# S5 chunk inputs in two products of 64 state columns instead of one of 128

## The chip, the cores and the metric

One core of a Trainium2 chip runs the whole program in one launch. The metric is the device time of one execution in microseconds (us), the median of several. The tensor engine (PE) multiplies a stationary operand that is loaded into it (the loads are shown as PEld) with a moving one and writes to PSUM. The vector engine (DVE), the scalar engine (ACT) and GpSimd (POOL) work elementwise, SyncE (SP) mostly issues DMAs.

## The reference, cut to what matters

Four decoder layers follow each other: S5, gated linear attention, differential attention, Mamba-2. The change touches the token mixer of the first, a diagonal complex state space model with 128 groups of 16 channels and 64 states. It runs over 256 tokens in chunks of 64.

```python
ug = u.reshape(bsz, nc, S5_CHUNK, S5_GROUPS, S5_GROUP)...
def chunk_step(carry, u_c):
    h_re, h_im = carry
    dr = jnp.einsum('tbgh,gph->tbgp', u_c, bb_re)
    di = jnp.einsum('tbgh,gph->tbgp', u_c, bb_im)
    pr, pim, sr, si = lax.associative_scan(_complex_affine_combine, (a_re, a_im, dr, di), axis=0)
    sr = sr + pr * h_re - pim * h_im
    si = si + pr * h_im + pim * h_re
    y = jnp.einsum('tbgp,ghp->tbgh', sr, c_re) - jnp.einsum('tbgp,ghp->tbgh', si, c_im)
    return (sr[-1], si[-1]), y
...
g = jax.nn.gelu(y)
out = g * jax.nn.sigmoid(g @ w_glu) * jax.nn.silu(z)
```

## The kernel before

The kernel works with chunks of four tokens: the inputs of a chunk, weighted with powers of the transition, give what the chunk adds to the state (the chunk input); the state at the chunks' starts follows from a recurrence over 64 chunks, and the outputs from the inputs within a chunk (matrix `tm`) and the state at its start (`E`). All of it is done in full fp32, which PE takes in two passes: every matmul in the code is two records in the trace.

The 2048 channels are worked through in four units of 512 (`s5_unit(ub)`), each in two parts, ahead of the `yield` and behind it. Ahead of it stand, for each of four sub-blocks `sb`:

- `scaled` on DVE (L651 to 656) makes the weighted input matrix `bu`; four ACT copies (L668) spread it into a padded tile `bpp`; eight PE transposes (L673) and two ACT copies (L674) make the stationary matrix `pm`, 128 x 128 for each of two complex parts `c` and four `g`;
- PE multiplies it with the inputs `V` (128 x 64) into `dps`, the chunk inputs, for two complex parts and four `g` (L678, eight matmuls, 16 records);
- three ACT copies (L681) put `dps` into `E`, in the order in which the recurrence reads it.

`psc` (L641) turns the output matrices once in a unit, with stationary operands of 64 columns, and ACT copies them into `ct` (L643). Then for each sub-block `cu` (DVE, one buffer) is copied to `cp` (ACT, L691), PE makes the output kernel `kps` (L695), and DVE and ACT copy it into `kt` (L698, L699). Sixteen DMAs on SP (L703) place the pieces of `kt` in `tm`. DVE then runs the recurrence over `E`: ten steps (L712 to 715) and eight large operations (L727 to 730). Behind the `yield` PE computes `y` from `V` and `tm` (L741) and from `E` and `cp` (L745), and ACT applies gelu (L747).

Between the two parts of a unit a list of other work is taken up, the fill: the input projection (L226), which makes the `V` of the later units (DVE transposes, L791), the gate and the queries. Its matmuls have 512 moving columns where weights stand still, 256 otherwise. A scheduler that gives each instruction a priority and follows estimated times sets the order on every engine; the parts of the units have a raised priority. Each engine then executes its list strictly in this order. PSUM buffers limit it: `ps` has three (shared by `psc`, transposes, `dps`, `kps`), `ps2` (for `y`) one, `acc` (fill) two. Behind the last unit the next projection starts (L228), which first needs fp32r halves of the normalised input (`hhi`, L821; `pr`, L822); `pr` reuses space that the last `y` matmuls read.

Of the kernel before, what the change touches and what calls it, by code (L numbers as in the profile page):

```python
# [37 lines left out]
class Net:  # L38
# [571 lines left out]
    def s5_unit(self, ub, V, p, tab, fix, gT):  # L610

        nc, a = self.nc, self.a
# [25 lines left out]
        for c in range(2):  # L638
            for r in range(4):
                for h in range(2):  # L640
                    nc.tensor.matmul(psc[64 * h:64 * h + 64, c, r, :], cnat[:, c, r, :], idv[:, :, h, :],  # L641
                                     start=True, stop=True)
        nc.scalar.copy(ct.rearrange("p r c g h -> p c r (g h)"), psc)  # L643

        def scaled(dst, src, tb, k, conj):

            sv = bc(src.rearrange("p c g h -> p (c g) h"), 2, 4)
            w1, w2 = (t_([P, 2, 4, 4, 16], f"q{i}") for i in range(2))
            for i, t in enumerate((w1, w2)):
                pw = tb[:, i, :, k].rearrange("p e c g -> p (c g) e")  # L650
                vec.tensor_tensor(t.rearrange("p c g e h -> p (c g) e h"), sv, bc(pw, 3, 16), MUL)  # L651
            vec.tensor_tensor(dst[:, 0], w1[:, 0], w2[:, 1], SUB)
            if conj:
                vec.scalar_tensor_tensor(dst[:, 1], w1[:, 1], -1.0, w2[:, 0], MUL, SUB)
            else:
                vec.tensor_tensor(dst[:, 1], w1[:, 1], w2[:, 0], ADD)
# [3 lines left out]
        for sb in range(4):  # L660
            l0 = 4 * sb
            ls = slice(l0, l0 + 4)
            bu = t_([P, 2, 4, 4, 16], "bu", 2)
            bpp = bpps[sb % 2]
            scaled(bu, bt[:, sb], pwb, 4 * ub + sb, False)
            for c in range(2):
                for ps_, hs_ in halves:
                    nc.scalar.copy(bpp[ps_, c, :, :, hs_], bu[ps_, c])  # L668
            pm = t_([P, 2, 4, P], "pm", 2)
            for c in range(2):  # L670
                tp = self.ps().rearrange("p (g x) -> p g x", g=4)
                for g in range(4):
                    nc.tensor.transpose(tp[:, g, :], bpp[:, c, g].rearrange("p s x -> p (s x)"), self.ident)  # L673
                nc.scalar.copy(pm[:, c], tp)  # L674
            dps = self.ps().rearrange("p (c g j) -> p c g j", c=2, g=4)
            for c in range(2):
                for g in range(4):
                    nc.tensor.matmul(dps[:, c, g, :], pm[:, c, g, :], V[:, :, l0 + g, :], start=True, stop=True)  # L678

            for d, s, n in ((32, 0, 32), (8, 32, 24), (1, 56, 7)):  # L680
                nc.scalar.copy(E[:, :, ls, d:d + n], dps[:, :, :, s:s + n])  # L681

        kt = t_([P, 4, P], "kt")
        for sb in range(4):
            l0 = 4 * sb
# [47 lines left out]
        for sb in range(4):  # L733
            l0 = 4 * sb
# [4 lines left out]
            for t in range(4):  # L739
                for g in range(4):  # L740
                    nc.tensor.matmul(y[32 * g:32 * g + 32, t, :], tm[:, l0 + g, 32 * t:32 * t + 32], V[:, :, l0 + g, :],  # L741
                                     start=True, stop=False)
                for c in range(2):
                    for g in range(4):
                        nc.tensor.matmul(y[32 * g:32 * g + 32, t, :], cp[:, c, g, t, :], E[:, c, l0 + g, :],  # L745
                                         start=False, stop=c == 1)
# [813 lines left out]
```

## Time and profile before

| | |
|---|---|
| runs | 1404.85, 1398.51, 1406.41 us; median 1404.85 |
| profiled execution | 1399.02 us, span 1397.0 us |
| PE busy | 1339.7 us, 96% of the span |
| PEld busy | 1089.2 us, 78% |
| DVE busy | 979.5 us, 70% |
| ACT busy | 765.3 us, 55% |
| POOL busy | 122.6 us, 9% |

The profiled execution is 5.83 us below the median of the runs. The S5 units run from about 38 to 237 us of the span. In the rows further below a time is counted from the start of the span, a busy time includes the tail of a group, so that consecutive rows of PE overlap a little, and what stands in brackets is idle time of the engine ahead of the row and what ended it.

### The profile page before, as it was taken

Reading aid. Unit: us, or ns where it says so; the run is one execution under the profiler, and the core shown is the slowest. Engines: PE = TensorE matmul, PEld = TensorE weight load, DVE = VectorE, ACT = ScalarE, POOL = GpSimd, SP = SyncE. Lnnn points to the kernel's source line nnn. Section 1 sums busy time; section 2 is a strip of 40 time slices with the busy share of each in tenths; the row PEclk is TensorE's granted clock in tenths of the full one; section 3 lists DMA queues with packets and bytes.
Section 4 is the critical chain, followed back from the end, with each engine's and each line's share of the span. In section 5 each row is a group of like instructions: output and inputs, shape, how many; then the busy total and the mean of one; then the engine's idle time right before and its main releaser. Section 6 shows DMA issues by size and latency. Waiting matters only on the chain. (4 is left out here: it accounts for less than half of the span.)

```text
span 1397.0 us, 24146 instructions
## 1 busy us (share of the span) xinstructions
PE 1339.7 (96%) x9482; PEld 1089.2 (78%) x9482; DVE 979.5 (70%) x1807; ACT 765.3 (55%) x1336; POOL 122.6 (9%) x153
## 2 busy tenths in 40 slices
PE   6999999999999899999999999999899999999998
PEld 3675667899988787786887777777777898888976
DVE  7689787876547577665467687676766587777873
ACT  2674543565543576554456566566555466665652
POOL 1320000010002100001012021102002000000000
PEclk9999999999999899999999999999999999999999
DMA  5444134565655465444655544344335454444342
GB/s 176 93 103 141 46 95 159 188 183 150 188 186 179 121 180 153 123 150 123 197 168 182 161 129 147 129 141 152 106 121 163 131 151 137 142 146 136 128 144 76
DMA packets 175666, 199.86 MB, mean 143 GB/s; under 512 B 32329, under 2 KB 112450, under 8 KB 175554
## 3 DMA queue, kind: packets, MB, share of 16 engines
q1 hardware_dynamic: 173442, 193.72, 45.5%
q10 hardware_dynamic: 1280, 3.21, 0.7%
q0 software_dynamic: 832, 1.41, 0.7%
q8 instruction: 74, 1.21, 0.4%
q14 instruction: 38, 0.31, 0.1%
HBM read 194.64 MB, written 1.05 MB: 140 GB/s over the span
## 5 line engine op out<-in xcount | busy, mean ns | idle before, releaser
L115 DVE TENSOR_TENSOR lo<-raw,hi 128x1024 fp32r<-128x1024 f32 x331 | 400.4, 1214 | 220.8 <-ACT hi L114 220.1
L114 ACT CAST hi<-raw 128x1024 fp32r<-128x1024 f32 x331 | 343.6, 1040 | 377.7 <-PE acc L230 229.3
L228 PE MATMUL acc<-hi,hT 128*128 128x512 f32 (+1 forms) x576 | 232.9, 404 | 1.9 <-ACT v L947 1.2
L230 PE MATMUL acc<-hi,hT 128*128 128x512 f32 (+1 forms) x576 | 227.8, 396 | 1.5 <-DVE hT L118 1.3
L229 PE MATMUL acc<-lo,hT 128*128 128x512 f32 (+1 forms) x576 | 227.3, 395 | 0.0
L107 POOL TENSOR_TENSOR rr<-rv,mhalf 128x2 f32<-128x2 f32 (+3 forms) x34 | 69.4, 2042 | 1020.5 <-DVE rv L105 970.4
L228 PEld LDWEIGHTS acc<-hi,hT 128*128 128x128 f32 x576 | 109.8, 191 | 29.0 <-issue 3.4
L230 PEld LDWEIGHTS acc<-hi,hT 128*128 128x128 f32 x576 | 109.5, 190 | 27.6 <-DVE hT L118 2.7
L229 PEld LDWEIGHTS acc<-lo,hT 128*128 128x128 f32 x576 | 109.6, 190 | 22.1 <-issue 0.2
L228 PE MATMUL ps<-hT,hi 128*128 128x256 f32 (+1 forms) x328 | 96.4, 294 | 3.9 <-DVE hT L118 1.4
L230 PE MATMUL ps<-hT,lo 128*128 128x256 f32 (+1 forms) x328 | 95.1, 290 | 0.1
L229 PE MATMUL ps<-hT,hi 128*128 128x256 f32 (+1 forms) x328 | 95.1, 290 | 0.0
L226 PE MATMUL acc<-raw,hT 128*128 128x512 f32 x160 | 76.8, 612 | 0.0
L228 PE MATMUL ps<-ghi,hi 128*128 128x256 f32 x256 | 72.6, 284 | 0.7 <-ACT xt L421 0.7
L229 PE MATMUL ps<-glo,hi 128*128 128x256 f32 x256 | 71.8, 281 | 0.0
L230 PE MATMUL ps<-ghi,lo 128*128 128x256 f32 x256 | 71.8, 281 | 0.0
L228 PEld LDWEIGHTS ps<-hT,hi 128*128 128x128 f32 (+1 forms) x328 | 63.0, 192 | 6.9 <-issue 2.1
L228 PE MATMUL acc<-hT,hi 128*128 128x256 f32 x224 | 64.7, 289 | 2.0 <-ACT xq L469 1.2
L230 PEld LDWEIGHTS ps<-hT,lo 128*128 128x128 f32 (+1 forms) x328 | 63.0, 192 | 1.3 <-issue 0.4
L230 PE MATMUL acc<-hT,lo 128*128 128x256 f32 x224 | 63.8, 285 | 0.0
L229 PEld LDWEIGHTS ps<-hT,hi 128*128 128x128 f32 (+1 forms) x328 | 63.0, 192 | 0.7 <-issue 0.2
L229 PE MATMUL acc<-hT,hi 128*128 128x256 f32 x224 | 63.5, 284 | 0.0
(481 smaller groups left out, 2802.6 us busy)
## 6 DMA issues: line engine op xcount, KB each, us to landing
raw<-in_w_out_dram SPq DMA_DIRECT2D x80, 512.0 KB, 3.7
raw<-in_diff_w_in_dram SPq DMA_DIRECT2D x72, 512.0 KB, 3.7
raw<-in_ssd_w_in_dram SPq DMA_DIRECT2D x56, 512.0 KB, 4.0
raw<-in_gla_w_in_dram SPq DMA_DIRECT2D x48, 512.0 KB, 3.7
raw<-in_s_w_in_dram SPq DMA_DIRECT2D x40, 512.0 KB, 4.8
raw<-in_w_mem_kv_dram SPq DMA_DIRECT2D x32, 512.0 KB, 4.0
raw<-in_s_w_glu_dram SPq DMA_DIRECT2D x32, 512.0 KB, 3.8
tm<-kt SPq DMA_DIRECT2D x16, 64.0 KB, 2.1
```

The lines of the kernel that those rows point to most:

```text
L107: nc.gpsimd.tensor_tensor(r, v, self.mhalf[:, :n], ALU.pow)
L114: nc.scalar.copy(hi, src)
L115: nc.vector.tensor_tensor(lo, src, hi.bitcast(F32), SUB)
L226: mm(out, s[0], m[0], start=start, stop=stop)
L228: mm(out, s[0], m[0], start=start, stop=False)
L229: mm(out, s[0], m[1], start=False, stop=False)
L230: mm(out, s[1], m[0], start=False, stop=stop)
```

## The change

Each of the eight matmuls that make `dps` becomes two, each with half of the 128 state columns of `pm` as its stationary operand, and into half of the partitions of `dps`. The sums are the same. In the four units 128 matmuls become 256, in records 256 become 512.

```diff
             dps = self.ps().rearrange("p (c g j) -> p c g j", c=2, g=4)
             for c in range(2):
                 for g in range(4):
-                    nc.tensor.matmul(dps[:, c, g, :], pm[:, c, g, :], V[:, :, l0 + g, :], start=True, stop=True)
+                    for q in (0, 64):
+                        nc.tensor.matmul(dps[q:q + 64, c, g, :], pm[:, c, g, q:q + 64], V[:, :, l0 + g, :],
+                                         start=True, stop=True)
```

The scheduler makes another order of all engines' work from it, from the second sub-block of unit 0 to the end of unit 3; behind that, and in the other three layers, the orders are equal. Lines behind L678 are two further down in the changed kernel. Numbers in names tell buffers apart.

PE in unit 0, around the first two sub-blocks (`ps_430`, `ps_466` or `ps_474` are `dps`, the other `ps` are transposes), before:

```order
L226 MATMUL acc_717<-raw_353,hT_134 128x512
L678 MATMUL ps_430<-V_355,pm_417 128x64 x8
L673 MATMUL ps_454<-ident,bpp_304 128x128 x4
L673 MATMUL ps_460<-ident,bpp_304 128x128 x4
L226 MATMUL acc_717<-raw_353,hT_134 128x512
L678 MATMUL ps_466<-V_355,pm_453 128x64 x8
```

and now:

```order
L226 MATMUL acc_749<-raw_353,hT_134 128x512
L679 MATMUL ps_430<-V_355,pm_417 64x64 x16
L673 MATMUL ps_462<-ident,bpp_304 128x128 x4
L673 MATMUL ps_468<-ident,bpp_304 128x128 x4
L226 MATMUL acc_749<-raw_353,hT_134 128x512
L679 MATMUL ps_474<-V_355,pm_461 64x64 x16
```

Here only the shape is another, and the count; the order is the same. From unit 1 on the sixteen often stand in two groups of eight with a fill matmul between them.

PE in unit 1, behind the chunk inputs: `kps` of the third sub-block (from `cp_291`; `acc` is fill), before:

```order
L695 MATMUL ps_1192<-cp_290,bpad 32x128 x4
L226 MATMUL acc_767<-hT_134,raw_740 128x256
L695 MATMUL ps_1192<-cp_290,bpad 32x128 x4
L226 MATMUL acc_767<-hT_134,raw_740 128x256 x2
L226 MATMUL acc_1329<-hT_119,raw_763 128x256
L695 MATMUL ps_1214<-cp_291,bpad 32x128 x8
L226 MATMUL acc_1329<-hT_119,raw_763 128x256 x3
```

and now:

```order
L697 MATMUL ps_1256<-cp_290,bpad 32x128
L226 MATMUL acc_1393<-hT_134,raw_797 128x256
L697 MATMUL ps_1256<-cp_290,bpad 32x128
L226 MATMUL acc_1393<-hT_134,raw_797 128x256 x2
L226 MATMUL acc_1393<-hT_119,raw_795 128x256 x4
L226 MATMUL acc_1393<-hT_134,raw_797 128x256 x4
L697 MATMUL ps_1278<-cp_291,bpad 32x128 x3
L226 MATMUL acc_1415<-hT_119,raw_1389 128x256
L697 MATMUL ps_1278<-cp_291,bpad 32x128
L226 MATMUL acc_1415<-hT_119,raw_1389 128x256
L697 MATMUL ps_1278<-cp_291,bpad 32x128
```

Its eight matmuls stood together, three fill matmuls behind the `kps` before it; now ten fill matmuls are ahead of its first, and one between each of the next. On DVE the copy of this `kps` into `kt` stands in the midst of unit 0's recurrence.

PE in unit 3, around the last `kps` (from `cp_292`), before:

```order
L678 MATMUL ps_2330<-V_1966,pm_2317 128x64 x8
L695 MATMUL ps_2354<-cp_289,bpad 32x128 x8
L695 MATMUL ps_2376<-cp_290,bpad 32x128 x8
L695 MATMUL ps_2398<-cp_291,bpad 32x128 x8
L695 MATMUL ps_2420<-cp_292,bpad 32x128
L226 MATMUL acc_2509<-raw_1952,hT_119 128x512
L695 MATMUL ps_2420<-cp_292,bpad 32x128
```

and now (`ps_258_2065` and `ps_259_2164` are `y` of unit 2):

```order
L226 MATMUL acc_2933<-hT_134,raw_2660 128x256
L697 MATMUL ps_2548<-cp_292,bpad 32x128
L743 MATMUL ps_258_2065<-V_1462,tm_302 32x64 x4
L747 MATMUL ps_258_2065<-E_294,cp_299 32x64 x8
...
L747 MATMUL ps_258_2065<-E_294,cp_299 32x64 x8
L697 MATMUL ps_2548<-cp_292,bpad 32x128 x7
L226 MATMUL acc_2933<-hT_134,raw_2660 128x256
L743 MATMUL ps_259_2164<-V_1462,tm_302 32x64 x4
```

The last `kps` of unit 3 moved behind the first half of unit 2's `y`. The fill that stood between unit 3's `y` matmuls is now all ahead of them.

ACT at the third sub-block of unit 3, before:

```order
L681 COPY E_295<-ps_2258 128x2x4x7
L674 COPY pm_2281<-ps_2282 128x512
L674 COPY pm_2281<-ps_2288 128x512
L681 COPY E_295<-ps_2294 128x2x4x32
L681 COPY E_295<-ps_2294 128x2x4x24
L681 COPY E_295<-ps_2294 128x2x4x7
```

and now:

```order
L683 COPY E_295<-ps_2362 128x2x4x7
L674 COPY pm_2393<-ps_2394 128x512
L693 COPY cp_290<-cu_2493 64x16x16
L469 COPY xq_2662<-acc_2637 128x1024
L674 COPY pm_2393<-ps_2400 128x512
L693 COPY cp_291<-cu_2515 64x16x16 x3
L683 COPY E_295<-ps_2406 128x2x4x32
L683 COPY E_295<-ps_2406 128x2x4x24
L683 COPY E_295<-ps_2406 128x2x4x7
```

All sixteen `cp` copies of unit 3 stood ahead of its first `E` copies; now they lie between them.

## Rows read from the trace of the kernel before

**Rows 1.** Busy time by stretch; stretch, length, then busy (count) per engine.
```profile
core 0: us, PE busy (x) PEld busy (x) DVE busy (x) ACT busy (x) POOL busy (x), PEclk, DMA share, GB/s
...
90.20:121.30 31.10, 31.10 (x201) 20.85 (x200) 30.50 (x70) 16.04 (x39) 2.11 (x3) 1.00 0.40 113
...
sum 188.80, PE 183.34 PEld 129.44 DVE 153.01 ACT 97.89 POOL 16.55; mean PE 18.33 PEld 12.94 DVE 15.30 ACT 9.79 POOL 1.66
```

**Rows 2.** Timeline of PE, unit 0: start, us, engine, line, operation, count.
```profile
52.00 1.89 PE L678 MATMUL ps<-V,pm 128*128 128x64 f32 x16
```

**Rows 3.** Timeline of all engines, unit 2: `psc` with columns of 64.
```profile
99.65 1.01 PEld L641 LDWEIGHTS ps<-ident,cnat 128*64 128x64 f32 x32 [0.20 <-issue]
99.65 1.15 PE L641 MATMUL ps<-ident,cnat 128*64 128x64 f32 x32
```

**Rows 4.** Timeline of ACT, unit 0: copies of the second chunk input.
```profile
53.93 0.70 ACT L681 COPY E<-ps 128x256 f32<-128x256 f32 x3
```

**Rows 5.** Timeline of all engines, end of unit 1's chunk inputs.
```profile
89.04 0.70 ACT L681 COPY E<-ps 128x256 f32<-128x256 f32 x3 [0.33 <-PE ps L678]
...
89.75 0.40 ACT L691 COPY cp<-cu 64x256 f32<-64x256 f32 x1
...
90.19 0.42 DVE L652 TENSOR_TENSOR cu<-q,q 128x256 f32<-128x256 f32 x1 [5.42 <-ACT cp L691]
```

**Rows 6.** Timeline of PE: fill alone, and fill with single `kps` matmuls between.
```profile
105.45 7.50 PE L226 MATMUL acc<-hT,raw 128*128 128x256 f32 x34
...
195.06 0.41 PE L695 MATMUL ps<-cp,bpad 128*32 128x128 f32 x2
195.39 1.13 PE L226 MATMUL acc<-raw,hT 128*128 128x512 f32 x2
196.45 0.41 PE L695 MATMUL ps<-cp,bpad 128*32 128x128 f32 x2
```

**Rows 7.** Timeline of DVE: recurrences of units 0 and 3.
```profile
120.37 0.96 DVE L730 TENSOR_TENSOR E<-E,fx 128x784 f32<-128x784 f32 x1
...
210.26 0.69 DVE L712 TENSOR_TENSOR sa<-E,s5tw 128x512 f32<-128x512 f32 x1
...
211.98 0.62 DVE L712 TENSOR_TENSOR sa<-E,s5tw 128x448 f32<-128x448 f32 x1
...
222.75 0.97 DVE L730 TENSOR_TENSOR E<-E,fx 128x784 f32<-128x784 f32 x1
```

**Rows 8.** Timeline of PE: unit 1's `y`, unit 3's first chunk input, the end.
```profile
159.95 0.32 PE L745 MATMUL ps<-E,cp 128*32 128x64 f32 x8
160.08 0.29 PE L741 MATMUL ps<-V,tm 128*32 128x64 f32 x8
...
160.42 0.29 PE L741 MATMUL ps<-V,tm 128*32 128x64 f32 x8
...
180.11 1.89 PE L678 MATMUL ps<-V,pm 128*128 128x64 f32 x16
...
232.84 2.86 PE L226 MATMUL acc<-hT,raw 128*128 128x256 f32 x12
...
236.73 0.38 PE L228 MATMUL ps<-hhi,hi 128*128 128x256 f32 x1 [1.03 <-ACT hi L114]
```

**Rows 9.** Timeline of ACT, unit 3: the last copies into `E`.
```profile
192.46 0.70 ACT L681 COPY E<-ps 128x256 f32<-128x256 f32 x3 [1.79 <-PE ps L678]
```

**Rows 10.** Groups by line, ACT, 47 to 237 us; count, busy, mean ns.
```profile
L691 ACT COPY cp<-cu 64x256 f32<-64x256 f32 x64 | 25.8, 403 | 18.8 <-PE ps L745 11.4 <-DVE cu L652 6.5
...
L674 ACT COPY pm<-ps 128x512 f32<-128x512 f32 x31 | 17.3, 606 | 0.4 <-PE ps L673 0.2
```

**Rows 11.** Timeline of SP: DMAs into `tm` of units 1 and 2.
```profile
111.73 10.69 SPq L703 DMA_DIRECT2D tm<-kt  x16
...
170.62 13.12 SPq L703 DMA_DIRECT2D tm<-kt  x16
```

**Rows 12.** Line L703 (all 64 DMAs into `tm`): from issue to landing.
```profile
DMA to landing us min/median/max: 1.8/2.1/3.8
```

## The prediction, made before the result was known

> **What bounds the kernel now.** I read the busy time by stretch first. From 47.9 to 236.7 us, where the changed matmuls lie, PE is busy 183.3 of 188.8 us [rows 1], so it idles 5.5 us. DVE is no bystander: from 90.2 to 121.3 us it is busy 30.5 of 31.1 us, as full as PE, on unit 0's recurrence and on the inputs of units 1 and 2 [rows 1]. ACT is third, but within the chunk inputs of a unit it is the full one: in unit 0 it starts its copies out of `dps` at 53.93 without a wait ahead of them [rows 4]. PE is filled up with work that may run at any time. So a busy PE doesn't yet say that PE sets the end: shorter work on PE moves the end only where a copy on ACT and a recurrence on DVE move with it. The end of the stage is the chain of unit 3: last copy into `E`, recurrence, `y`, fill, next projection at 236.73 [rows 7 to 9]. All behind it has the same order before and after, so I price the change by the shift of this one start.
>
> **The matmuls alone.** The sixteen records of one sub-block take 1.89 us [rows 2]. The changed shape occurs already: `psc` has stationary operands of 64 columns and 64 moving ones, and 32 of its records take 1.15 us [rows 3]. The saving is 0.74 us a sub-block, 16 x 0.74 = 11.8 us in all. That is the upper end; the lower end is no gain, if the halves don't overlap as those of `psc` do. I take the `psc` row: same columns, rows and type, and it too writes the two halves of the partitions in turn; it differs in that the same stationary columns come twice in a row.
>
> There is a page that speaks against it. The row shows 32 weight loads of 64 columns in 1.01 us, 32 ns each, under matmuls that end with them [rows 3]. The Trainium skill, "TensorE: Matmul & The Clock Gate", section "LDWEIGHTS (loading the stationary operand)", puts a load at its columns over 1.2 in ns, 53 ns for 64, and its Part 3 lets a load overlap running matmuls only in other row groups, which these halves don't use. As an estimate from that page 32 loads take 1.7 us and the gain is near nothing. The measured 32 ns decides; the case stays below as a rival.
>
> **What the new order adds on PE.** Over the stage it changes between instructions of different column counts 164 times instead of 127, since fill and short matmuls alternate more. A pair of single `kps` records and one fill matmul takes 196.45 - 195.06 = 1.39 us [rows 6]; fill alone takes 7.5/17 = 0.44 us for 256 columns, so 0.88 for 512 [rows 6]. The interruption costs 0.5 us, of which two changes take some 0.22 each. 37 more cost 8.1 us. On PE alone the net is 11.8 - 8.1 = 3.7 us less. It becomes time only if nothing else is later.
>
> **Unit 0.** ACT is full here, and its copies are not fewer. PE's gain turns into waiting for ACT, but for the last sub-block: 0.7 us.
>
> **Unit 1.** DVE stood 5.42 us until 90.19, for a `cp` copy that lay behind the last copies into `E`, which themselves waited 0.33 us for `dps` [rows 5]. Now all four first `cp` copies lie ahead of these: 0.33 + 0.70 = 1.0 us, and up to two and a half shorter `dps` (1.9 us) before: 2.9 us. DVE starts again at 87.3. It loses that by another wait. The copy of the third `kps` into `kt` is the 38th of some 70 instructions that take 30.5 us [rows 1], so it is due at 87.3 + 16.6 = 103.9. On PE this `kps` now lies behind 27 fill matmuls (11.9 us), twelve interruptions (6 us) and 1.8 us of `kps` and `y`, and ends at 87.2 + 19.7 = 106.9. Behind it on DVE wait the rest of unit 0's recurrence and the transposes of `V`. The recurrence ended at 121.3 [rows 7]; I take 121.9, from 118.4 (no wait) to 123.
>
> **Unit 2.** DVE has its `V` transposes earlier in the order, by some 3 us of work, and loses half of it to PE's later `y`. The dps then hang on ACT and PE in turn, where shorter `dps` count in full. I carry 0.85 us into unit 1's `y`: it starts at 159.1 instead of 159.95 [rows 8].
>
> **Unit 3, start.** Before, its `psc` and first transposes were strewn among unit 1's `y`. Now they lie behind all of it: 16 quarters of 0.34 us (160.42 - 160.08, [rows 8]), 5.4 us; 14 fill matmuls of 512 columns, 12.3 us; eight interruptions, 3.1 us. That is 20.8 us, to 179.9. With the transposes and their copies the first `dps` comes at 182.6 instead of 180.11 [rows 8], 2.5 us later.
>
> **Unit 3, ACT.** The sixteen `cp` copies stood ahead of the chunk inputs and now lie in them. From 181 on ACT has there 16 `cp`, 8 `bpp` and 4 `bpad` copies of the same shape, 28 x 0.403 = 11.3 us; 8 `pm` copies of 0.55 to 0.61, 4.6 us; 4 x 0.70 = 2.8 us into `E`; and some 1.7 us for three others [rows 9, 10]. That is 20.4 us, so the last copy into `E` ends at 201.4, where it was 193.2 [rows 9]: 8.2 us later. The `cp` come from `cu` on DVE, which now stands behind unit 2's whole recurrence; that one ends by 182 (158, where unit 1's is done and its `y` can start, + 23.7 as worked out next), so ACT and not DVE sets this.
>
> **Unit 3, recurrence.** It no longer shares DVE with unit 2's. A step takes 1.72 us, and from the eighth on 223.7 - 212.0 = 11.7 us are left [rows 7], so 7 x 1.72 + 11.7 = 23.7 us alone, to 225.1. In it DVE waits for the last `kps`, due at about 217 and made by PE only behind half of unit 2's `y` and some 24 fill matmuls, at about 219.5: 2.4 us more. The end is 227.5 against 223.7, 3.8 us later. What was 8.2 us late wins 4.4 back.
>
> **Unit 3, the DMAs.** The last piece of `kt` comes at 219.9 instead of early in the recurrence, and only then can sixteen DMAs fill `tm`. SP issues one per 10.69/16 = 0.67 us or 13.12/16 = 0.82 us, and a landing takes 2.1 us, at most 3.8 [rows 11, 12]. I take the faster row, as SP has nothing ahead then: 219.9 + 15 x 0.67 + 2.1 = 232.0. Every quarter of `y` needs pieces of `tm`, the fourth needs them all. The remaining 13 quarters (4.4 us) and a wait for gelu, 0.4 us, give 236.8 for the end of `y`, against 232.84 [rows 8]. No fill is left to put between. The casts, which need the last `y` out of the way, and the next projection follow by the same distance: 240.7 against 236.73, 4.0 us later.
>
> **Sum.** Taken along this chain: +2.5 (start), +5.7 (ACT), -4.4 (recurrence alone and its wait), and +0.2 as `tm` ends the chain in place of `E`: **+4.0 us**, 1403.0 against the profiled 1399.0. The profiled execution lies 5.8 us below the median of the runs, 1404.85; on that scale I expect **1409 us**.
>
> **Rivals.** *PE sets the stage after all.* For it speaks that PE idles only 5.5 of 188.8 us [rows 1], so the fill bridges what I call waits, and the later `kps` costs nobody. Then the end moves by PE's own net, -3.7 us (1401), and if the changes of column count hide behind loads, by up to -11.8 us (1393). Against it: at the end no fill is left.
>
> *The tail of `tm` is longer*, and the kernel slower. If the DMAs run at 0.82 us each and land in 3.8 us [rows 11, 12], because weight loads for the next projection are in the queues, the last piece lands at 219.9 + 12.3 + 3.8 = 236.0, 4.0 us later, and everything behind with it: +8.0 us, 1413. It decides from the point where the last landing comes after 235, which makes +7 us.
>
> *The halves don't overlap.* Then the change doesn't do what it says: 16 sub-blocks take their 1.89 us or more, unit 1 and 2 give back what I credited (2.9 and 0.85 us), and the 37 column changes stay. Added to the forecast that is +4 to +12, I take 1414.
>
> **Chances.** Forecast, between -2 and +6 us, 0.53; PE alone 0.18, of which 0.11 below -7 us; the longer tail 0.19; no overlap 0.10. About 0.5%, 7 us, is what a measurement of this kernel tells from no change. Faster 0.11; slower 0.27, from the last two less what stays under 7 us, here 0.04, plus 0.02 for a forecast short by that much; same 0.62. The range reaches from the nearer end of the first rival to beyond the last: 1398 to 1417.
>
> **What would show it.** Right: `dps` groups near 1.15 us; ACT's last copy into `E` of unit 3 about 201; the last `kps` about 219; a run of sixteen DMAs into `tm` from about 220; PE idle, 4 to 8 us, ahead of the last `y`; the projection from 240.7. Wrong: `dps` groups at 1.9 us (no overlap); the last `kps` by 210, or unit 3's `y` ending before 230, which would let PE's gain through; ACT with pauses in unit 3, which would put DVE or PE in its place.

## The result, and the profile after

The changed kernel takes 1411.64 us (median of 11 runs, 1406.16 to 1414.56), the kernel before beside it 1400.31 us (11 runs). The ratio over all runs is 1.007 with a 95% interval of 1.0057 to 1.0082: slower by 0.7%; the two medians differ by 11.3 us. The forecast was 4 us slower, 1409 us, and "no change", within 0.5%, the likeliest class. The time lies in the range of 1398 to 1417; the change lies outside the forecast's own -2 to +6 us, and the class was the wrong one. That 1411.64 is within 3 us of 1409 is luck: 1409 was reckoned from a median of three runs, 1404.85, and the eleven runs have 1400.31.

The profiled execution took 1406.16 us, span 1404.2. It is the fastest of its eleven; another profiled one of the same kernel, further down, took 1412.39 and is nearer to the median. The lines below answer to those of before. PE first: the chunk inputs of one sub-block of unit 0 (32 records), then unit 1's `y`, unit 3's first chunk input, its last `kps`, and the end.

```profile
50.56 1.17 PE L679 MATMUL ps<-V,pm 128*64 128x64 f32 x32
...
159.53 0.32 PE L747 MATMUL ps<-E,cp 128*32 128x64 f32 x8
...
183.91 0.69 PE L679 MATMUL ps<-V,pm 128*64 128x64 f32 x16
...
219.93 0.53 PE L697 MATMUL ps<-cp,bpad 128*32 128x128 f32 x11
...
233.34 0.32 PE L743 MATMUL ps<-V,tm 128*32 128x64 f32 x1 [0.24 <-DMA tm<-kt]
...
234.66 0.44 PE L743 MATMUL ps<-V,tm 128*32 128x64 f32 x8 [0.47 <-ACT gT L749]
234.87 0.65 PE L747 MATMUL ps<-E,cp 128*32 128x64 f32 x16
235.30 0.44 PE L743 MATMUL ps<-V,tm 128*32 128x64 f32 x8
...
237.95 0.44 PE L743 MATMUL ps<-V,tm 128*32 128x64 f32 x8 [0.50 <-ACT gT L749]
...
240.81 0.32 PE L743 MATMUL ps<-V,tm 128*32 128x64 f32 x8 [0.52 <-ACT gT L749]
...
245.94 0.38 PE L228 MATMUL ps<-hhi,hi 128*128 128x256 f32 x1 [3.48 <-ACT hi L114]
```

The chunk inputs went from 1.89 to 1.17 us [rows 2], as `psc` had shown [rows 3]. Yet the next projection starts at 245.94 instead of 236.73 [rows 8], 9.2 us later. Up to 219.93 every stop is within 1.5 us of its forecast. What differs is the last part: a quarter of `y`, one of the four steps of a sub-block with eight records of L743 and sixteen of L747 (from 234.66 to 235.30), takes 0.64 us where it took 0.34 [rows 8], and between the groups of four quarters PE waits for gelu, since no fill is left.

DVE: the restart in unit 1, the third `kps` into `kt`, the end of unit 0's recurrence, then start, last `kt` and end of unit 3's, and the cast `pr` that waits for the last `y` matmuls.

```profile
86.20 0.42 DVE L652 TENSOR_TENSOR cu<-q,q 128x256 f32<-128x256 f32 x1 [2.39 <-ACT cp L693]
...
106.16 0.25 DVE L700 SCALAR_TENSOR_TENSOR kt<-i,gains,ps 128x32 f32<-128x32 f32 x1 [4.00 <-PE ps L697]
...
121.93 0.96 DVE L732 TENSOR_TENSOR E<-E,fx 128x784 f32<-128x784 f32 x1
...
201.93 0.69 DVE L714 TENSOR_TENSOR sa<-E,s5tw 128x512 f32<-128x512 f32 x1 [1.83 <-ACT E L683]
...
220.52 0.25 DVE L700 SCALAR_TENSOR_TENSOR kt<-i,gains,ps 128x32 f32<-128x32 f32 x1 [2.08 <-PE ps L697]
...
227.37 0.97 DVE L732 TENSOR_TENSOR E<-E,fx 128x784 f32<-128x784 f32 x1
...
242.28 0.76 DVE L824 TENSOR_TENSOR pr<-hT,hhi 128x256 fp32r<-128x256 f32 x2 [13.53 <-PE ps L743]
```

ACT's last copies into `E` and SP's transfers into `tm` for unit 3, to be read against [rows 9] and [rows 11]:

```profile
201.23 0.67 ACT L683 COPY E<-ps 128x256 f32<-128x256 f32 x3
```

```profile
220.80 11.25 SPq L705 DMA_DIRECT2D tm<-kt  x16
```

Busy time by stretch over this end (columns as in [rows 1]):

```profile
228.00:232.00 4.00, 2.83 (x56) 2.02 (x58) 0.75 (x3) 0.00 (x0) 0.00 (x0) 0.68 0.23 50
232.00:238.00 6.00, 4.56 (x134) 3.60 (x128) 0.00 (x0) 0.77 (x2) 0.00 (x0) 0.50 0.33 96
238.00:246.00 8.00, 4.00 (x193) 3.68 (x193) 3.72 (x14) 1.93 (x4) 0.00 (x0) 0.89 0.27 93
```

From 232 to 238 us the granted clock is 0.50, TensorE's level of 1.2 GHz, after PE had waited for the recurrence and for pieces of `tm`. Before, it stayed at 1.00 there, also in the stretch in which PE waited for the casts:

```profile
236.00:238.00 2.00, 0.51 (x3) 0.31 (x3) 2.00 (x5) 2.00 (x3) 0.00 (x0) 1.00 1.01 394
```

### The profile page after: what moved, and what is told of

The parts are those of the page before. It is cut to its first block, busy times and chain, and to the rows that moved or that the text cites. A ratio compares the mean times of both kernels' runs of the same rounds, so it can differ in the third digit from the quotient of the medians.

```text
span 1404.2 us, 24654 instructions
## 1 busy us (share of the span) xinstructions
PE 1337.9 (95%) x9738; PEld 1077.3 (77%) x9738; DVE 981.1 (70%) x1807; ACT 764.1 (54%) x1336; POOL 119.7 (9%) x153
## 5 line engine op out<-in xcount | busy, mean ns | idle before, releaser
L228 PE MATMUL ps<-hT,hi 128*128 128x256 f32 (+1 forms) x328 | 94.1, 287 | 3.9 <-DVE hT L118 1.4
L229 PE MATMUL ps<-hT,hi 128*128 128x256 f32 (+1 forms) x328 | 93.0, 283 | 0.0
```

Of the source, the lines that this page charges most:

```text
L228: mm(out, s[0], m[0], start=start, stop=False)
L229: mm(out, s[0], m[1], start=False, stop=False)
```

## The experiments

The two times of a row are from one chip and one series. In the kernels with a held order (all but those with priority 300 and the changed kernel again) a list of instruction numbers at the end of the file fixes what each engine issues in the S5 stage (a dependency between neighbours that adds no wait on a semaphore). Beside the edit that is named with each, two such kernels then differ in the list alone. The ratios are over all runs and not of the two medians; the last two columns are from the profiled execution.

| kernel | us | before | ratio, 95% interval | first chunk input at | projection at |
|---|---|---|---|---|---|
| halves, order of before | 1396.02 | 1403.34 | 0.9939, 0.9915 to 0.9962 | 50.29 | 232.29 |
| whole products, new order | 1420.05 | 1403.34 | 1.0108, 1.0084 to 1.0132 | 50.11 | 256.39 |
| last `kps` early | 1416.85 | 1403.34 | 1.009, 1.0064 to 1.0116 | 48.95 | 249.73 |
| added products in the tail | 1413.55 | 1403.34 | 1.0068, 1.0044 to 1.0091 | 47.18 | 245.95 |
| last `kps` in the middle | 1411.14 | 1403.12 | 1.0058, 1.0038 to 1.0077 | 48.81 | 245.50 |
| halves, priority 300 | 1391.07 | 1403.12 | 0.991, 0.9889 to 0.9931 | 47.55 | 226.28 |
| whole products, priority 300 | 1401.79 | 1403.12 | 0.9996, 0.9977 to 1.0015 | 46.85 | 236.30 |
| two queues | 1408.66 | 1400.23 | 1.0056, 1.004 to 1.0072 | 50.14 | 245.25 |
| two queues, added products | 1407.93 | 1400.23 | 1.0052, 1.0036 to 1.0067 | 48.05 | 243.72 |
| changed kernel again | 1411.65 | 1400.23 | 1.0077, 1.0059 to 1.0096 | 49.02 | 249.06 |

Executions reach the S5 stage at different times: the first chunk input of unit 0 starts at 47.89 in the profiled execution before, and at 47.42 and 49.02 in the two of the changed kernel. From there to the projection it is 236.73 - 47.89 = 188.8 us before and 198.5 and 200.0 us in the changed kernel. What lies behind the projection, where the orders are equal, takes 1158.2 to 1166.9 us, so a profiled execution's time and its projection need not move together.

### The matmuls and the order, each alone

```diff
         getattr(net, f"layer{i}")()
+        if i == 0:
+            hold_order(tc)
```

This line stands in both kernels. The first has the changed kernel's matmuls and the list of before, the second the matmuls of before and the list of the changed kernel.

> The two products of 64 columns, with every engine held to the order of the kernel before. Order theory: the loss comes from the new order alone, so this is not slower than before; PE saves 16 x 0.74 = 11.8 us in the chunk inputs, most of it is absorbed where ACT or DVE is full, and the next projection starts 0 to 4 us earlier than 236.73: ratio to before 0.996 to 1.001. Shape theory: the smaller products cost by themselves (column changes, waits between halves, a lower clock), ratio 1.004 to 1.01 as in the changed kernel.

> The whole products of 128 columns, with every engine held to the order of the changed kernel. Order theory: as slow as the changed kernel or slower, since the chunk inputs of unit 3 take 4 x 0.74 us more on top of its late start: next projection at 246 to 249, ratio to before 1.007 to 1.012. Shape theory: back to before, ratio 0.998 to 1.002.

The halves in the old order are faster than the kernel before by 7.3 us; the whole products in the new order are slower by 16.7 us. Both lie on the side of the order theory and beyond its numbers: it had a ratio of 0.996 or more for the first, and the projection of the second by 249. ACT and PE with the halves in the old order:

```profile
186.72 0.70 ACT L683 COPY E<-ps 128x256 f32<-128x256 f32 x3 [1.26 <-PE ps L679]
```

```profile
232.29 0.38 PE L228 MATMUL ps<-hhi,hi 128*128 128x256 f32 x1 [1.58 <-ACT hi L114]
```

The last copy into `E` starts 5.7 us earlier than before [rows 9]; the wait for PE ahead of it is shorter, 1.26 against 1.79. At the projection 4.4 us are left; but this execution reached its first chunk input 2.4 us later than before, and from there to the projection it takes 182.0 instead of 188.8 us, 6.8 less, near the 7.3 of the medians. So the matmuls do what they were priced for, and part of the gain, some 7 of 11.8 us, reaches the end. The groups by line show what the new order costs PE. PE from 47 to 262 us, whole products in the new order:

```profile
L226 PE MATMUL acc<-hT,raw 128*128 128x256 f32 x192 | 54.1, 402 | 0.0
L226 PE MATMUL acc<-raw,hT 128*128 128x512 f32 x102 | 49.6, 609 | 0.0
...
L695 PE MATMUL ps<-cp,bpad 128*32 128x128 f32 x256 | 18.0, 279 | 0.0
L641 PE MATMUL ps<-ident,cnat 128*64 128x64 f32 x96 | 3.5, 225 | 0.3 <-ACT kt L699 0.3
```

The kernel before, same stretch:

```profile
L226 PE MATMUL acc<-raw,hT 128*128 128x512 f32 x102 | 51.1, 620 | 0.0
L226 PE MATMUL acc<-hT,raw 128*128 128x256 f32 x192 | 49.1, 392 | 0.0
...
L695 PE MATMUL ps<-cp,bpad 128*32 128x128 f32 x256 | 13.7, 279 | 0.0
...
L641 PE MATMUL ps<-ident,cnat 128*64 128x64 f32 x96 | 6.5, 230 | 0.0
```

The first three groups, the same instructions, take 121.7 instead of 113.9 us: 7.8 us more. The estimate for 37 more changes of column count was 8.1. But `psc` (L641), which now stands together, takes 3.0 us less, and in such sums the tails of broken-up groups count twice, as they overlap what follows. All of PE is busy 190.92 us from the first chunk input to the projection, before 183.35: 7.6 us more, of which some 2.4 are quarters of `y` at the low clock, as counted below for the changed kernel. So the order costs PE some 5 us with whole products. With the halves it is 184.58 (the changed kernel) against 174.81 (the order of before), 9.8 us more, or some 7 without the low clock.

### The tail of unit 3

Two theories were put to the test: that the late `kps` with its transfers makes the end late, and that the low clock does. The first kernel moved the last `kps` of unit 3, its copies and its transfers forward in the new order; the second keeps PE busy.

```diff
 L226 MATMUL acc_2902<-hT_119,raw_2646 128x256 x2
+L697 MATMUL ps_2548<-cp_292,bpad 32x128 x8
 L743 MATMUL ps_258_2065<-V_1462,tm_302 32x64
...
-L697 MATMUL ps_2548<-cp_292,bpad 32x128
...
-L697 MATMUL ps_2548<-cp_292,bpad 32x128 x7
```

> The changed kernel with its order, but for 32 instructions: the last kps of unit 3 on PE behind four fill matmuls instead of twenty-odd, its four copies into kt on DVE and ACT and the sixteen DMAs into tm at the front of the recurrence. Tail theory: the DMAs start near 208 instead of 220.8, the recurrence loses its wait of 2.1 us and ends at 226.2, y of unit 3 ends at 233 to 235 instead of 242.3 without a fall of the clock, and the next projection starts at 237 to 239 instead of 245.9; ratio to before 0.998 to 1.003. Against it: if the late start of unit 3 or the order as a whole is the cause, y moves by the 2.1 us alone, ratio 1.005 or more.

It was a miss. DVE, then PE:

```profile
210.96 0.56 DVE L700 SCALAR_TENSOR_TENSOR kt<-i,gains,ps 128x32 f32<-128x32 f32 x3 [5.87 <-DMA tm<-kt]
```

```profile
211.58 1.08 PE L697 MATMUL ps<-cp,bpad 128*32 128x128 f32 x16 [4.72 <-ACT kt L701]
```

`kt` is one buffer, and unit 2's transfers were still reading it. DVE stood 5.87 us in the midst of the recurrence, and the whole was slower. So its time tells nothing of either theory, only that with one `kt` the tail cannot come forward further than those transfers allow. Its trace tells a little: PE has no wait for a piece of `tm` behind the recurrence, and from there to the cast `pr` it is 245.24 - 233.50 = 11.7 us, where the changed kernel takes 13.9 and the kernel before 9.0.

```diff
+            if ub == 3:
+                self.busy(2 if sb == 0 else 1)
...
+            self.nc.tensor.matmul(self.idle[:, :256], self.ident, self.warm, start=True, stop=True)
```

> The changed kernel with its order, and 21 products of 256 columns more whose sums nobody reads, put on PE where it waits between 226 and 246 us. Clock theory: the granted clock stays at 1.0 there, the quarters of y take 0.34 us instead of 0.64, and the projection behind runs at full clock: 4 to 7 us less than the changed kernel, ratio to before 1.000 to 1.005. If the waits alone cost the time: the same as the changed kernel or up to 2 us more, ratio 1.007 to 1.009.

Stretches of this kernel:

```profile
220.00:230.00 10.00, 8.56 (x245) 6.02 (x237) 8.09 (x11) 1.98 (x5) 0.00 (x0) 1.00 0.24 54
230.00:240.00 10.00, 8.24 (x269) 6.09 (x272) 0.00 (x0) 0.77 (x2) 0.00 (x0) 1.00 0.27 70
```

and its PE at the last transfer:

```profile
235.58 0.24 PE L747 MATMUL ps<-V,tm 128*32 128x64 f32 x1 [1.44 <-DMA tm<-kt]
```

The clock is 1.00 throughout, and the projection starts at 245.95 as without. The last transfer landed 2.2 us later in this execution, which took what the clock gave. The ratio, 1.0068, is that of the changed kernel within the noise (1.0044 to 1.0091). The clock alone is not the cause.

> The changed kernel in its own order, but for the tail of unit 3: the last output kernel stands behind the second quarter of unit 2's output on PE instead of behind the eighth, its first three copies into kt stand on DVE behind the sixth step of unit 3's recurrence and the fourth behind the eighth, those of ACT ahead of unit 2's gelu, and the sixteen transfers into tm ahead of three weight loads. Nothing else moves, and no work is left out. Theory (the late kps and its transfers set the end of layer 0): DVE has no wait of 2 us in the recurrence, which ends at about 226.2 instead of 228.3; the transfers are issued from about 216 to 227 and the last lands at about 229.5 instead of 233.3; the last output ends at about 236 instead of 242.3, and the next projection starts at about 239.5 instead of 245.9. Against the kernel before 0.999 to 1.004, against the changed one some 5 us less. Rival (all of unit 3 starts late, by the copies into E that lie behind cp, and the tail only follows): the recurrence ends within 1 us of 228.3, the output within 2 us of 242.3, and the ratio stays at 1.005 or above.

The list moves eight matmuls on PE (16 records), four copies on DVE, two on ACT and sixteen transfers on SP. As a diff of PE's order:

```diff
 L747 MATMUL ps_258_2065<-E_294,cp_298 32x64 x8
+L697 MATMUL ps_2548<-cp_292,bpad 32x128 x8
 L226 MATMUL acc_2933<-hT_134,raw_2660 128x256
...
-L697 MATMUL ps_2548<-cp_292,bpad 32x128
...
-L697 MATMUL ps_2548<-cp_292,bpad 32x128 x7
```

PE at the last transfer and at the last quarter of `y`, and DVE:

```profile
231.36 0.31 PE L743 MATMUL ps<-V,tm 128*32 128x64 f32 x1 [0.33 <-DMA tm<-kt]
...
240.40 0.25 PE L743 MATMUL ps<-V,tm 128*32 128x64 f32 x3 [1.75 <-issue]
...
245.50 0.58 PE L228 MATMUL ps<-hhi,hi 128*128 128x256 f32 x1 [4.24 <-ACT hi L114]
```

```profile
203.32 0.69 DVE L714 TENSOR_TENSOR sa<-E,s5tw 128x512 f32<-128x512 f32 x1 [1.83 <-ACT E L683]
...
226.49 0.97 DVE L732 TENSOR_TENSOR E<-E,fx 128x784 f32<-128x784 f32 x1
...
241.09 0.76 DVE L824 TENSOR_TENSOR pr<-hT,hhi 128x256 fp32r<-128x256 f32 x2 [13.22 <-PE ps L743]
```

The wait of 2 us in the recurrence is gone, and the last landing is 2 us earlier, though unit 3's recurrence began 1.4 us later in this execution. It bought 0.4 us at the projection, 1.8 counted from the recurrence's start: waits for gelu, the low clock (0.66 from 230 to 235) and a pause of 1.75 us for which the trace names only "issue" took its place. The ratio, 1.0058, overlaps that of the changed kernel, and lies where the rival had it, that unit 3 is late as a whole.

To compare executions whose unit 3 begins at different times, the end of the recurrence is the mark: from there to the cast `pr` it is 242.28 - 228.34 = 13.9 us in the changed kernel, 13.6 here, 9.3 in the forecast, and before 232.72 - 223.72 = 9.0 [rows 7]:

```profile
232.72 0.76 DVE L822 TENSOR_TENSOR pr<-hT,hhi 128x256 fp32r<-128x256 f32 x2 [8.59 <-PE ps L741]
```

The next edit gives seven of the sixteen transfers to ACT's queue:

```diff
-                nc.sync.dma_start(...
+                (nc.scalar if ub == 3 and 4 * s + g in (1, 3, 5, 7, 9, 11, 13) else nc.sync).dma_start(...
```

> The changed kernel in its own order, but seven of unit 3's sixteen transfers into tm are issued by ACT (three behind its last copy into kt, three and one behind unit 2's next outputs) and nine by SP. Nothing is left out. It takes the late landing away and leaves the granted clock, the waits for gelu and the late recurrence. Theory (the landings set the end of unit 3's output): the last landing is at about 229.3 instead of 233.3, the output starts behind the recurrence at 228.3 and ends at about 238.5 instead of 242.3, the projection starts at about 242 instead of 245.9; ratio to the kernel before 1.002 to 1.005, the changed one beside it 1.005 to 1.009. Rival (the clock at 1.2 GHz and the waits for gelu take the place of the landings): projection at 244.5 or later, and no difference from the changed kernel beside it above 0.2%.

The kernel after it has this edit and the added products together, the third is the changed kernel as it is.

> The same with the 21 added products of 256 columns that nothing reads, in the waits of unit 3's output; no other work is added and none left out. It takes the late landing and the low clock away together. If each hides behind the other: last landing about 229.3, clock 1.00 from 222 on, quarters of the output 0.34, its end at about 236.5 and the projection at about 240; ratio to before 1.000 to 1.003. Rival (the late recurrence of unit 3 and the four outputs that follow it without fill are what is late): the projection at 243 or later, ratio 1.005 or above.

> The changed kernel once more, on the same chip as the two beside it, as their measure: by every theory 1.005 to 1.009 of the kernel before, projection at about 246.

DVE with two queues, then the changed kernel again:

```profile
229.73 0.97 DVE L732 TENSOR_TENSOR E<-E,fx 128x784 f32<-128x784 f32 x1
...
240.86 0.76 DVE L824 TENSOR_TENSOR pr<-hT,hhi 128x256 fp32r<-128x256 f32 x2 [9.74 <-PE ps L743]
```

```profile
228.47 0.98 DVE L732 TENSOR_TENSOR E<-E,fx 128x784 f32<-128x784 f32 x1
...
244.20 0.76 DVE L824 TENSOR_TENSOR pr<-hT,hhi 128x256 fp32r<-128x256 f32 x2 [14.35 <-PE ps L743]
```

PE of the changed kernel again, the last transfer and the projection:

```profile
235.36 0.32 PE L743 MATMUL ps<-V,tm 128*32 128x64 f32 x1 [0.25 <-DMA tm<-kt]
...
249.06 0.58 PE L228 MATMUL ps<-hhi,hi 128*128 128x256 f32 x1 [4.69 <-ACT hi L114]
```

Behind the recurrence two queues need 240.86 - 230.70 = 10.2 us, the changed kernel beside it 244.20 - 229.45 = 14.8. The stretches with two queues:

```profile
228.00:232.00 4.00, 2.05 (x96) 1.56 (x96) 3.05 (x5) 0.38 (x1) 0.00 (x0) 1.00 0.25 50
232.00:236.00 4.00, 3.01 (x156) 2.62 (x158) 0.00 (x0) 0.77 (x2) 0.00 (x0) 1.00 0.47 137
```

In this execution the clock stays at 1.00 there with no work added. In time it is 3.0 us (1411.65 to 1408.66), just above the 0.2% that was to tell the two theories apart, and less than the ratio that the theory wanted; the projection, 245.25, lies where the rival had it, though from its own first chunk input it is 195.1 us against 200.0 in the kernel beside it. The intervals of the two ratios overlap, so the 3 us are not clear of noise. The landings are probably one cause: worth 4.6 us behind the recurrence in these two executions, some 3 us by the medians, and the low clock went with them. The added products on top bring 0.7 us, less than can be told apart, and that kernel ended where its rival had it: ratio 1.0052, projection at 243.72. Some of their own time lies in the chain there. With the transfers on two queues 8.4 us remain against the kernel before; the recurrence of unit 3 ends 4.8 to 7.0 us later than before in these three executions [rows 7], and 4.6 to 4.7 in each when it is counted from the first chunk input.

### An order that keeps the gain

```diff
-                        with tc.high_priority(offset=200):
+                        with tc.high_priority(offset=300):
```

in both places where a unit's parts are begun, once with halves and once with whole products.

> The changed kernel with one number changed: the raised priority of the S5 units is 300 instead of 200, so that the scheduler makes another order. In it all sixteen cp copies of unit 3 lie ahead of its first copies into E, its four output kernels stand together right behind its last chunk input, as in the kernel before, and fill is kept between its output matmuls. Nothing is left out. Theory (the halves save 4 to 10 us and the order that came with them cost more): dps groups 1.15 us, the last copy into E of unit 3 by 193, the last output before 233, projection between 230 and 236; ratio to the kernel before 0.990 to 0.998. Rival (the halves help only in the order of the kernel before): projection at 240 or later, ratio 1.002 or more.

> The kernel before with the same one number, 300 instead of 200: whole products, in the order that the scheduler makes for them with it. Nothing is left out. It is the control of the run beside it. If the gain there is the halves', this one lies at 0.999 to 1.004 of the kernel before, and the halves are 4 us or more shorter at the same number. If the gain is the number's, this one lies within 0.2% of the halves with it, at 0.990 to 0.998.

With halves it is faster than both kernels: 1391.07 us, 0.991 of before. The number alone does nothing (0.9996). Halves and whole products differ by 10.7 us at this priority, nine tenths of the 11.8 that the prediction had as the upper end; but the scheduler made an order for each of them, so this is not the halves' gain alone, which was 7.3 in the held order of before. DVE, ACT and PE of the halves with priority 300, at unit 3's end:

```profile
210.07 0.97 DVE L732 TENSOR_TENSOR E<-E,fx 128x784 f32<-128x784 f32 x1
```

```profile
184.77 0.70 ACT L683 COPY E<-ps 128x256 f32<-128x256 f32 x3 [1.75 <-PE ps L679]
```

```profile
221.19 5.45 PE L226 MATMUL acc<-hT,raw 128*128 128x256 f32 x24
226.28 0.47 PE L228 MATMUL ps<-hhi,hi 128*128 128x256 f32 x1
```

The copies into `E` are done at 185.5, the recurrence at 211.04, 17.3 us ahead of the changed kernel, and 12 fill matmuls (24 records) are left behind `y` to cover the casts. The last row has no wait ahead of it.

## Why the prediction was right and wrong

**The matmuls: right.** 1.15 was taken, 1.17 measured for 32 records, 37 ns for a load and its matmul. By the Trainium skill ("TensorE: Matmul & The Clock Gate", section "LDWEIGHTS (loading the stationary operand)") a load of 64 columns takes 53 ns, by which, as an estimate, the gain would be near nothing; the trace, with 37 ns, does not agree. "The halves don't overlap" falls.

**PE's net: taken too large.** 11.8 us less for the matmuls and 8.1 more for the order were taken, 3.7 less in all. By PE's whole busy time from the first chunk input to the projection the halves save 8.5 us in the order of before (174.81 instead of 183.35), and the order costs some 5 to 7. The changed kernel has 184.58, 1.2 us more than before, or 1.2 less without the low clock's 2.4.

**Units 0 to 2: right within about 1 us.** DVE's restart 86.20 (forecast 87.3), the third `kps` 106.16 (106.9), unit 0's recurrence done at 122.9 (121.9), unit 1's `y` at 159.53 (159.1). What unit 1 gained was indeed lost again to the wait of 4.00 us.

**Unit 3 up to the recurrence: right, a little short.** First chunk input 183.91 (182.6; its eight interruptions were entered as 3.1 us, and at the prediction's own 0.5 each they are 4.0, which gives 183.5), last copy into `E` ends at 201.9 (201.4), last `kps` at 220.46 (219.5), recurrence ends at 228.3 (227.5). That PE sets the stage after all thereby falls: its gain does not reach the end.

**The DMAs and unit 3's output: the step that failed.** The steps behind the recurrence were sized at 9.3 us, and measured 13.9. The last landing was taken at 232.0 and came at 233.3 (0.70 us a transfer instead of 0.67, from a start 0.9 later). From there 4.8 us were taken, 13 quarters of 0.34 and one wait of 0.4 for gelu; it took 9.0. Thirteen quarters at 0.34 are 4.4; some eight of them ran at the low clock with 0.64 instead, 2.4 more; and three gaps for gelu, 0.7 each from quarter to quarter, took 2.1. The prediction saw that no fill was left and took the speed of the quarters from rows with fill between them [rows 8]. It had no row on the clock, and counted one gelu wait of the three that the single buffer of `ps2` makes behind the last landing. So the chain was the right one, and its term for the output was 4.6 us too small.

**The scale.** The profiled execution of after was the fastest of its runs, so its +9.2 at the projection is low. In the other one it is 249.06 - 236.73 = 12.3, which splits by the same steps into the forecast's 4.0; 1.6 for a later start of the recurrence; 0.3 in it; 5.4 behind it; 1.0 in the casts. Of the 1.6, 1.1 lie ahead of the stage, whose first chunk input came at 49.02 instead of 47.89. Without them it is 11.2, and the medians differ by 11.3.

**The longer tail**, the rival with +8, had the right place: in that execution the last piece landed at 235.36, beyond the 235 from which it was to decide, at 12.18/16 = 0.76 us each. But a transfer took no 3.8 us to land, the last some 2, and weight loads were not needed for it: SP issued its next one behind the sixteen, and the last one ahead of them 4.6 us before the first. Two queues, which undo it, give back only some 3 us.

**The chances.** The forecast's own range, up to +6, missed. The errors of the likeliest case lay on one side, which was not counted: in unit 3 each step came later than taken, by 0.5 to 1.3 us up to the recurrence's end, and the output by 4.6 more.

**What stays open.** That the 8 us which two queues leave are mostly the late recurrence (4.7 us in the trace) and the output without fill (1.2, 10.2 against 9.0) is read from the trace and not tested one by one; only orders as wholes were compared. Unit 3's recurrence starts between 201.79 and 204.30 us in executions that share the order up to there. Counted from the first chunk input it is 154.0 to 154.6 us in all of them, so the spread comes from ahead of the changed matmuls; why the stage begins up to 3 us apart there was not tried.

## What to carry to other kernels

Under a scheduler that follows estimated times, an edit of one instruction is two changes: the instruction, and the order of every engine around it. Measure them apart by holding the order, and when the instruction gains and the order loses, look for another order before giving the edit up (here 1411.6 became 1391.1 us with one number). Read a stage in two executions from its own first row, as they can reach it some us apart. A tail in which no fill is left must be priced with the engine's idle rows, every buffer wait and the low clock, and not with rows from a filled stretch.

## What the runs showed of the hardware

- The granted clock fell to 0.50 (1.2 GHz) from 230 us on, behind PE's waits for gelu, the recurrence and transfers, and made a quarter of `y` 0.64 instead of 0.34 us. With extra products that nothing reads it stayed at 1.00, and so it did from 228 to 236 us in the one profiled execution with two queues.
- PE paused 0.6 to 1.75 us in the midst of unit 2's and unit 3's small matmuls with no releaser but "issue", in most of these kernels, halves and whole products alike. Their cause was not tried.
- ACT issued three transfers into `tm` in 2.06 us and the next three in 3.03, 0.69 and 1.01 each; SP needed 0.70 and 0.76 in the two executions of the changed kernel.

```profile
223.44 2.06 ACTq L705 DMA_DIRECT2D tm<-kt  x3
...
226.25 3.03 ACTq L705 DMA_DIRECT2D tm<-kt  x3
```
